# Token-major retention values, gate and memory values with 512 features per matmul

## The chip, the cores and the metric

The kernel runs on one core of one Trainium2 chip. The metric is the device time in microseconds (us) of one execution, the median of several runs. The core has five engines that work side by side, each through its own queue in order: PE (TensorE, matmuls; the profile lists its weight loads apart as PEld), DVE (VectorE), ACT (ScalarE), POOL (GpSimd) and SP (SyncE, which issues most DMAs here).

## The reference

The program is a trunk of two layers over 256 tokens of 1024 features. Each layer has a mixer (a retention branch and a convolution branch, merged by gates), a cross-attention into 256 memory tokens, and a gated MLP. What the change touches:

```python
p = u @ w_in                                  # u: 256 tokens x 1024, normalised
q, k, v, g_ret, c_in, gates = jnp.split(p, cuts, axis=-1)
...
o = head_group_norm(chunk_retention(q, k, v), ret_gn_g)   # 4 heads, 512 values each
y_a = (jax.nn.silu(g_ret) * o) @ w_ret_out
...
k, v = jnp.split(mem_n @ w_xkv, 2, axis=-1)   # 256 memory tokens, 1024 keys, 1024 values
```

The group norm ends with a gain per feature, `ret_gn_g`, that multiplies beside the gate silu(g_ret).

## The kernel before

**Arithmetic.** All large products are in float32 by three matmuls in the one-pass float type (fp32r): each operand is split into a high and a low part, and high x high, high x low and low x high are summed in PSUM. `split` (lines 160 to 163) makes the parts with one ACT copy and one DVE subtraction; for weights the same stands in `prepare` (lines 125 to 133: tiles `raw`, `whi`, `wlo`).

**Weight stream.** Weights come as chunks of 128 partitions x 2048 numbers (1 MB). A chunk is two units of 1024 columns. `run` (lines 135 to 151) goes through a list of steps; it keeps up to four units split ahead of the step in hand (`UNITS`), four chunks on their way (`RAWS`), and after each step deals out some background work, in the mixer the 31 taps of the depthwise convolution (ACT products L488, DVE sums L491, tiles `prod` and `blk`). A scheduler that estimates times sets each engine's final order from that program order; `urgent` functions go ahead.

**Two ways to multiply.** `feat` (L171 to L173) has a weight block as the stationary operand and streams 256 tokens past it, so that the result is feature-major: features on partitions, tokens along the free axis. `tok` (L181 to L183) has 128 tokens of the activation as the stationary operand and streams 256 weight columns past them: the result is token-major. A chunk takes 48 matmuls of 128x256 either way: 8 k tiles x 3 products x 2 feature or token tiles. A `tok` step needs both units of its chunk for the first token tile and both again for the second.

**PSUM.** Step results go to four rotating banks, tag `mm`, one bank (2 x 256 numbers per partition) a step.

**Retention.** For each head: chunks of q, k (`feat`), two chunks of values v (`tok`), two chunks of the gate g (`feat`, silu on eviction, L590), then `scores` and `attend` (token-major result, group norm, tile `o`), and later `gate` (lines 559 to 574): eight transposes of `o` on PE (L563), the product with gain and gate on DVE (L571), and a split into `y`.

**Cross-attention.** `mem_v` (lines 447 to 454) makes the memory values in four `tok` chunks, each evicted by a split (L162, L163) on its own, between the steps of the four attention heads.

Of the kernel before, what the change touches and what calls it, by code (L numbers as in the profile page):

```python
# [7 lines left out]
F32 = mybir.dt.float32  # L8
# [3 lines left out]
ALU = mybir.AluOpType  # L12

P = 128
# [13 lines left out]
# columns of the parameter block, per layer (the final gain follows the layers)  # L28
# [11 lines left out]
# first chunks of the parts of the input projection: q, k, v, retention gate, convolution, merge gates  # L40
Q0, K0, V0, G0, C0, S0 = 0, 4, 8, 16, 24, 32

RAWS = 4        # chunks of weights on their way from DRAM
UNITS = 4       # half chunks kept split
BLOCKS = 10     # [128, 8, 256] tiles
TEMPS = 8       # [128, 2, 256] tiles
ROT_BY = 20     # units of the first layer over which the rotary tables are made
CONV_END = 1    # chunk of the retention output by which the taps are done
MEM_AT = 6      # chunk of the retention output after which the memory is normalised
# [6 lines left out]
def urgent(fn):  # L56
    """ahead of the weights still to be split"""
    def wrapped(self, *args, **kwargs):
        with self.tc.high_priority():
            return fn(self, *args, **kwargs)  # L60
    return wrapped


class Trunk:
# [37 lines left out]
    def step(self, fn, *units):  # L102
        """units: (chunk in DRAM, first column, k tiles, columns per k tile)"""
        self.steps.append((fn, units))
        self.planned += len(units)
# [5 lines left out]
    def token_pair(self, name, layer, c):  # L111
        src = self.io[name][layer, c]
        return (src, 0, 4, 256), (src, 1024, 4, 256)
# [39 lines left out]
    def spread_out(self, by):  # L153
        """work to be spread evenly over the steps up to unit number by"""
        work = {"items": [], "by": by, "due": 0.0}
        self.background.append(work)
        return work

# [1 line left out]
    def split(self, src, hi, lo):  # L160
        """src = hi + lo exactly, both rounded to the width of one pass."""
        self.nc.scalar.activation(hi, src, AF.Copy)  # L162
        self.nc.vector.tensor_tensor(lo, src, hi.bitcast(F32), op=ALU.subtract)  # L163

    def feat(self, out, w, u, k0=0, first=True, last=True):
        """out[feature, token] += sum_k w[k, feature] u[k, token]"""
        (wh, wl), (uh, ul) = w, u
        kt = wh.shape[1]
        for k in range(kt):
            a, b = first and k == 0, last and k == kt - 1  # L170
            self.nc.tensor.matmul(out, wh[:, k, :], uh[:, k0 + k, :], start=a, stop=False)  # L171
            self.nc.tensor.matmul(out, wh[:, k, :], ul[:, k0 + k, :], start=False, stop=False)  # L172
            self.nc.tensor.matmul(out, wl[:, k, :], uh[:, k0 + k, :], start=False, stop=b)  # L173

    def tok(self, out, ws, t, u):
        """out[token, feature] = sum_k u[k, token] w[k, feature]"""
        uh, ul = u
        ts = slice(t * P, t * P + P)
        for k in range(KT):
            wh, wl = (x[:, k % 4, :] for x in ws[k // 4])  # L180
            self.nc.tensor.matmul(out, uh[:, k, ts], wh, start=k == 0, stop=False)  # L181
            self.nc.tensor.matmul(out, uh[:, k, ts], wl, start=False, stop=False)  # L182
            self.nc.tensor.matmul(out, ul[:, k, ts], wh, start=False, stop=k == KT - 1)  # L183
# [6 lines left out]
    def tok_sum(self, parts):  # L190
        """per token: sum over partitions and over the parts, tokens on partitions"""
        ps = self.bank("nrm", 1)
        for i in range(2):
            for j, t in enumerate(parts):
                self.nc.tensor.matmul(ps[:, 0, i:i + 1], t[:, i * P:i * P + P], self.ones[:, 0:1],
                                      start=j == 0, stop=j == len(parts) - 1)
        return ps

    def spread(self, pending):
        """one value per token onto every partition, tokens along the free axis"""  # L200
        ps, col = pending
        for t in range(2):
            self.nc.tensor.matmul(ps[:, 1, t * P:t * P + P], col[:, t:t + 1].to_broadcast([P, P]), self.ident,
                                  start=True, stop=True)
        return ps[:, 1, :]
# [7 lines left out]
    def ssq_add(self, k, n, h):  # L213
        """squares of n feature tiles from tile k on; those of the last pair are left to the final sum"""
        nc, q = self.nc, self.temp()
        nc.scalar.activation(q[:, :n, :], h, AF.Square)
        last = self.gain == "final"
        if last and k >= 6:
            self.ssq += [q[:, i, :] for i in range(n)]
            return  # L220
        if k and n == 2:
            a = self.temp()
            nc.vector.tensor_tensor(a, self.ssq, q, op=ALU.add)
            q = a
        elif k:
            nc.vector.tensor_tensor(self.ssq[:, k % 2, :], self.ssq[:, k % 2, :], q[:, 0, :], op=ALU.add)
            q = self.ssq
        self.ssq = [self.halves(q)] if k + n == (6 if last else KT) else q
# [4 lines left out]
    def begin(self, gain=None):  # L233
        """before a residual is produced; with a gain, h times the gain is kept split as well, for
        the products that start before the norm is known"""
# [21 lines left out]
    def both(self, ps, w, u, midway=None):  # L257
        """two feature tiles side by side, k tile by k tile"""
# [13 lines left out]
    def each(self, ps, w, u, midway=None):  # L272
        """two feature tiles side by side, one after the other"""
# [11 lines left out]
    def ahead(self, chunks, normalise):  # L285
        """the first chunks after a norm work on the gained h; their results wait for the scale"""
# [92 lines left out]
    def rotary_tables(self):  # L379
        """angle in turns, reduced exactly, then sine and cosine; a list of small pieces"""  # L380
# [17 lines left out]
        def product(part, c, most, f, r):  # L398
            """acc += the part of a turn in part * c, where |part| <= most"""
# [26 lines left out]
    def memory(self, layer):  # L426
        """normalised memory, split; K and V follow as steps"""
# [19 lines left out]
    def mem_v(self, layer, c):  # L447
        def fn(*w):
            ps = self.bank()
            for t in range(2):  # L450
                self.tok(ps[:, t, :], w, t, self.mem)
            at = slice(c * 256, c * 256 + 256)
            self.split(ps, *(by_token(x)[:, :, at] for x in self.xv))
        self.step(fn, *self.token_pair("w_xkv", layer, 4 + c))

# [1 line left out]
    def mixer(self, layer):  # L457
# [19 lines left out]
        # convolution branch: the products of a tap on ScalarE, the sums on VectorE  # L477
# [40 lines left out]
        # retention  # L518
# [19 lines left out]
        def attend(h):  # L538
            s, v = X["s", h], X["v", h]
            for n in range(2):  # L540
# [15 lines left out]
                nc.scalar.activation(o, ps, AF.Identity, scale=rs, bias=nm)  # L556
                X["o", h, n] = o

        def gate(h):
# [7 lines left out]
            for j in range(2):  # L567
                y = self.temp()
                for i in range(2):
                    f = 2 * j + i  # L570
                    nc.vector.scalar_tensor_tensor(y[:, i, :], pt[j][:, i, :],  # L571
                                                   self.par("ret_gn_g", L, 4 * h + f),
                                                   X["g", h][:, f, :], op0=ALU.mult, op1=ALU.mult)
                self.split(y, hi[b][:, r + 2 * j:r + 2 * j + 2, :], lo[b][:, r + 2 * j:r + 2 * j + 2, :])

        def v_step(h, j):
            def fn(*w):
                ps = self.bank()
                for t in range(2):
                    self.tok(ps[:, t, :], w, t, X["u"])  # L580
                if j == 0:
                    X["v", h] = self.small([2, 512], "v", bufs=1)
                nc.scalar.activation(X["v", h][:, :, j * 256:(j + 1) * 256], ps, AF.Copy)
            self.step(fn, *self.token_pair("w_in", L, V0 + 2 * h + j))

        def ev_g(h, j):
            def fn(ps):
                if j == 0:
                    X["g", h] = self.small([4, N], "g", bufs=1)
                nc.scalar.activation(X["g", h][:, 2 * j:2 * j + 2, :], ps, AF.Silu)  # L590
            return fn
# [12 lines left out]
        g = lambda h: [in_step(G0 + 2 * h + j, ev_g(h, j)) for j in range(2)]  # L604
# [19 lines left out]
        # gates  # L624
# [17 lines left out]
        # retention output  # L642
# [43 lines left out]
        # convolution output and merge  # L686
# [29 lines left out]
    def cross(self, layer):  # L716
# [19 lines left out]
        def three(out, a, b, first, last):  # L736
            """out += a.T @ b, both split"""
# [155 lines left out]
def _turns():  # L893
    """1/(2 pi) in pieces of twelve bits"""
# [106 lines left out]
```

## Time and profile before

| What | Value |
| --- | --- |
| median of 3 runs | 1309.79 us (1309.69 to 1309.8) |
| profiled execution, span from first to last instruction | 1308.2 us |
| outside the span, median less span | 1.6 us |
| PE busy | 1290.4 us (99%) |
| DVE busy | 973.9 us (74%) |
| ACT busy | 852.2 us (65%) |
| mean granted TensorE clock | 0.997 |

The page gives no time of the profiled execution but its span; the 1.6 us between it and the median is taken as what lies around the span. A matmul's row has its duration with its passage through the array; matmuls overlap, so what one costs is the distance between the starts of neighbours, read from the timeline.

### The profile page before, as it was taken

The numbers are of one execution on the slowest core, as the hardware profiler recorded it, in microseconds if no ns is written. First come the engines' busy times: TensorE is split into PE (matmuls) and PEld (weight loads), VectorE is DVE, ScalarE is ACT, GpSimd is POOL, SyncE is SP. The second block draws the span as 40 slices with busy tenths as digits, with TensorE's granted clock in tenths as the row PEclk, the third lists the DMA queues.
The fourth block names the chain that finished last, engine by engine and source line by source line (L and its number), as shares of the span: only waits on it lengthen the run. The fifth ranks groups of instructions, "written<-read, shape, count | busy, mean of one in ns | idle before, by whom it ended". The sixth has DMA issues, their size and how long they took to land.

```text
span 1308.2 us, 25199 instructions
## 1 busy us (share of the span) xinstructions
PE 1290.4 (99%) x10592; PEld 1277.0 (98%) x10592; DVE 973.9 (74%) x1283; ACT 852.2 (65%) x1348; POOL 24.0 (2%) x31
## 2 busy tenths in 40 slices
PE   7999999999999999999999999999999999999997
PEld 6999999999999999999999999999999999999997
DVE  7989998767676588665677999985686757876643
ACT  5898899664455457654469898886544545666542
POOL 0000000000000000000000010000000000000000
PEclk9999999999999999999999999999999999999998
DMA  8554445455544345454555444445645444455450
GB/s 301 197 190 142 156 155 191 165 205 182 193 166 158 131 169 212 170 182 178 187 191 175 179 146 162 154 155 191 226 164 191 164 154 153 175 193 175 158 185 33
DMA packets 33089, 227.45 MB, mean 174 GB/s; under 512 B 3920, under 2 KB 4176, under 8 KB 6736
## 3 DMA queue, kind: packets, MB, share of 16 engines
q1 hardware_dynamic: 32688, 225.32, 47.9%
q8 instruction: 83, 1.36, 0.4%
q10 hardware_dynamic: 288, 0.52, 0.1%
q14 instruction: 30, 0.25, 0.0%
HBM read 224.78 MB, written 1.05 MB: 173 GB/s over the span
## 4 chain that ended last, share of the span: by engine, by line
PE 84%; issue 14%; DMA 1%; DVE 0%; SPq 0%; POOLq 0%; POOL 0%; DVEq 0%
PE mm L171 22%; PE mm L172 22%; PE mm L173 22%; PE mm L181 4%; PE mm L183 4%; PE mm L182 4%; PE mm L266 3%; PE att L542 1%; PE att L739 1%; PE att L740 1%; PE att L738 1%; DMA h<-in_x_dram 1%; PE att L563 1%; PE att L531 1%; PE att L544 1%
## 5 line engine op out<-in xcount | busy, mean ns | idle before, releaser
L171 PE MATMUL mm<-blk,whi 128*128 128x256 f32 x2880 | 817.0, 284 | 0.0
L173 PE MATMUL mm<-blk,wlo 128*128 128x256 f32 x2880 | 814.9, 283 | 0.0
L172 PE MATMUL mm<-blk,whi 128*128 128x256 f32 x2880 | 814.8, 283 | 0.0
L130 ACT ACTIVATE whi<-raw 128x1024 fp32r<-128x1024 f32 (+1 forms) x424 | 442.9, 1048 | 376.4 <-PE mm L172 289.3
L131 DVE TENSOR_TENSOR wlo<-raw,whi 128x1024 fp32r<-128x1024 f32 (+1 forms) x424 | 511.9, 1212 | 204.6 <-ACT whi L130 202.0
L171 PEld LDWEIGHTS mm<-blk,whi 128*128 128x128 f32 x2880 | 552.0, 192 | 2.2 <-issue 1.7
L172 PEld LDWEIGHTS mm<-blk,whi 128*128 128x128 f32 x2880 | 552.2, 192 | 1.7 <-issue 1.7
L173 PEld LDWEIGHTS mm<-blk,wlo 128*128 128x128 f32 x2880 | 552.0, 192 | 0.5 <-DVE wlo L131 0.2
L488 ACT ACTIVATE prod<-blk,params 128x255 f32<-128x255 f32 (+14 forms) x480 | 197.1, 487 | 1.8 <-DVE blk L491 1.7
L491 DVE TENSOR_TENSOR blk<-blk,prod 128x1020 f32<-128x1020 f32 (+14 forms) x120 | 138.4, 1153 | 15.3 <-ACT prod L488 14.6
L182 PE MATMUL mm<-wlo,blk 128*128 128x256 f32 x384 | 109.1, 284 | 0.0
L181 PE MATMUL mm<-whi,blk 128*128 128x256 f32 x384 | 108.9, 284 | 0.0
L183 PE MATMUL mm<-whi,blk 128*128 128x256 f32 x384 | 108.6, 283 | 0.0
L183 PEld LDWEIGHTS mm<-whi,blk 128*128 128x128 f32 x384 | 73.5, 191 | 0.0
L182 PEld LDWEIGHTS mm<-wlo,blk 128*128 128x128 f32 x384 | 73.5, 191 | 0.0
L181 PEld LDWEIGHTS mm<-whi,blk 128*128 128x128 f32 x384 | 73.4, 191 | 0.0
L162 ACT ACTIVATE blk<-t 128x512 fp32r<-128x512 f32 (+1 forms) x87 | 52.1, 616 | 17.3 <-DVE t L253 12.9
L163 DVE TENSOR_TENSOR blk<-t,blk 128x512 fp32r<-128x512 f32 (+1 forms) x87 | 57.7, 678 | 2.6 <-ACT blk L162 2.6
L266 PE MATMUL mm<-blk,whi 128*128 128x256 f32 x192 | 39.7, 299 | 8.1 <-ACT whi L130 8.1
L266 PEld LDWEIGHTS mm<-blk,whi 128*128 128x128 f32 x192 | 33.1, 207 | 8.1 <-ACT whi L130 8.1
L842 DVE SCALAR_TENSOR_TENSOR t<-t,params,t 128x255 f32<-128x255 f32 (+1 forms) x88 | 38.2, 478 | 0.0
L328 DVE TENSOR_TENSOR h<-mm,h 128x512 f32<-128x512 f32 (+1 forms) x26 | 16.9, 650 | 21.1 <-PE mm L173 16.0
(133 smaller groups left out, 747.2 us busy)
## 6 DMA issues: line engine op xcount, KB each, us to landing
raw<-in_w_in_dram SPq DMA_DIRECT2D x79, 1024.0 KB, 4.8
raw<-in_w_up_dram SPq DMA_DIRECT2D x44, 1024.0 KB, 4.8
raw<-in_w_ret_out_dram SPq DMA_DIRECT2D x16, 1024.0 KB, 4.8
raw<-in_w_xkv_dram SPq DMA_DIRECT2D x16, 1024.0 KB, 4.8
raw<-in_w_down_dram SPq DMA_DIRECT2D x16, 1024.0 KB, 4.8
raw<-in_w_conv_out_dram SPq DMA_DIRECT2D x8, 1024.0 KB, 4.8
raw<-in_w_mix_out_dram SPq DMA_DIRECT2D x8, 1024.0 KB, 4.8
raw<-in_w_xq_dram SPq DMA_DIRECT2D x8, 1024.0 KB, 4.8
```

The source lines that it names most:

```text
L130: nc.scalar.activation(hi[:, :n], raw, AF.Copy)
L131: nc.vector.tensor_tensor(lo[:, :n], raw, hi[:, :n].bitcast(F32), op=ALU.subtract)
L163: self.nc.vector.tensor_tensor(lo, src, hi.bitcast(F32), op=ALU.subtract)
L171: self.nc.tensor.matmul(out, wh[:, k, :], uh[:, k0 + k, :], start=a, stop=False)
L172: self.nc.tensor.matmul(out, wh[:, k, :], ul[:, k0 + k, :], start=False, stop=False)
L173: self.nc.tensor.matmul(out, wl[:, k, :], uh[:, k0 + k, :], start=False, stop=b)
L181: self.nc.tensor.matmul(out, uh[:, k, ts], wh, start=k == 0, stop=False)
L182: self.nc.tensor.matmul(out, uh[:, k, ts], wl, start=False, stop=False)
L183: self.nc.tensor.matmul(out, ul[:, k, ts], wh, start=False, stop=k == KT - 1)
L266: mm = lambda x, y, a, b: self.nc.tensor.matmul(out, x[:, k, :], y[:, k, :], start=a, stop=b, skip_group_check=True)
L488: nc.scalar.activation(t[:, i, :m], X["c"][:, k, :m], AF.Copy, scale=self.par("conv_dw_w", L, k * TAPS + TAPS - 1 - s))
L491: nc.vector.tensor_tensor(cc, cc, t[:, :, :m], op=ALU.add)
```

## The change

Three products change; q, k, the convolution, the merge gates and all later products keep their form.

1. `tok` streams 512 weight columns per matmul, and gets both token tiles at once, each with a whole PSUM bank as its output. A chunk now holds 4 of the 8 k tiles for 512 features (was 8 k tiles for 256); two chunks make 512 features. Each takes 24 matmuls of 128x512.
2. v and the memory values use it; two banks are held over two steps, and evicted after the second one. The memory values' split therefore comes after every second chunk.
3. The retention gate g becomes token-major too (it was `feat`). The gate multiplies the normalised `o` in `attend` before the transposes, and `gate` only applies the gain while it splits: one ACT copy with a scale and one DVE instruction per 128 features.

The host lays the chunks out to match. The file also loses its comments, so that line numbers move: `feat` is L172 to L174 and `tok` L185 in the changed kernel.

```diff
-        return (src, 0, 4, 256), (src, 1024, 4, 256)
+        return (src, 0, 2, 512), (src, 1024, 2, 512)
...
-    def tok(self, out, ws, t, u):
+    def tok(self, outs, ws, u, half):
         uh, ul = u
-        ts = slice(t * P, t * P + P)
-        for k in range(KT):
-            wh, wl = (x[:, k % 4, :] for x in ws[k // 4])
-            self.nc.tensor.matmul(out, uh[:, k, ts], wh, start=k == 0, stop=False)
-            self.nc.tensor.matmul(out, uh[:, k, ts], wl, start=False, stop=False)
-            self.nc.tensor.matmul(out, ul[:, k, ts], wh, start=False, stop=k == KT - 1)
+        for i, (wh, wl) in enumerate(ws):
+            for j in range(2):
+                k = 4 * half + 2 * i + j
+                for t, out in enumerate(outs):
+                    ts = slice(t * P, t * P + P)
+                    mm = lambda a, b, p, q: self.nc.tensor.matmul(out, a[:, k, ts], b[:, j, :], start=p, stop=q)
+                    mm(uh, wh, k == 0, False)
+                    mm(uh, wl, False, False)
+                    mm(ul, wh, False, k == KT - 1)
+    def flat_banks(self):
+        return [self.bank().rearrange("p t n -> p (t n)") for _ in range(2)]
...
     def mem_v(self, layer, c):
         def fn(*w):
-            ps = self.bank()
-            for t in range(2):
-                self.tok(ps[:, t, :], w, t, self.mem)
-            at = slice(c * 256, c * 256 + 256)
-            self.split(ps, *(by_token(x)[:, :, at] for x in self.xv))
+            if c % 2 == 0:
+                self.xv_ps = self.flat_banks()
+            self.tok(self.xv_ps, w, self.mem, c % 2)
+            if c % 2:
+                at = slice(c // 2 * 512, c // 2 * 512 + 512)
+                for t in range(2):
+                    self.split(self.xv_ps[t], *(by_token(x)[:, t, at] for x in self.xv))
...
                 nc.scalar.activation(o, ps, AF.Identity, scale=rs, bias=nm)
+                nc.vector.tensor_tensor(o, o, X["g", h][:, n, :], op=ALU.mult)
...
-            for j in range(2):
-                y = self.temp()
-                for i in range(2):
-                    f = 2 * j + i
-                    nc.vector.scalar_tensor_tensor(y[:, i, :], pt[j][:, i, :],
-                                                   self.par("ret_gn_g", L, 4 * h + f),
-                                                   X["g", h][:, f, :], op0=ALU.mult, op1=ALU.mult)
-                self.split(y, hi[b][:, r + 2 * j:r + 2 * j + 2, :], lo[b][:, r + 2 * j:r + 2 * j + 2, :])
+            for f in range(4):
+                src, gain = pt[f // 2][:, f % 2, :], self.par("ret_gn_g", L, 4 * h + f)
+                yh, yl = hi[b][:, r + f, :], lo[b][:, r + f, :]
+                nc.scalar.activation(yh, src, AF.Copy, scale=gain)
+                nc.vector.scalar_tensor_tensor(yl, src, gain, yh.bitcast(F32), op0=ALU.mult, op1=ALU.subtract)
...
+        def token_step(nm, at, fun, h, j):
             def fn(*w):
                 if j == 0:
+                    X[nm, "ps"] = self.flat_banks()
+                self.tok(X[nm, "ps"], w, X["u"], j)
+                if j:
+                    X[nm, h] = self.small([2, 512], nm, bufs=1)
+                    for t in range(2):
+                        nc.scalar.activation(X[nm, h][:, t, :], X[nm, "ps"][t], fun)
+            self.step(fn, *self.token_pair("w_in", L, at + 2 * h + j))
...
-        g = lambda h: [in_step(G0 + 2 * h + j, ev_g(h, j)) for j in range(2)]
+        g = lambda h: [token_step("g", G0, AF.Silu, h, j) for j in range(2)]
```

How the order changes is shown at three places. On PE, before, at the start of the second head's values in the first layer (`mm_1383` is the PSUM bank of its first 256 features; `whi_1268`/`wlo_1269` and `whi_1272`/`wlo_1273` are the chunk's two units; `blk_322` and `blk_323` the parts of the activation):

```order
L181 MATMUL mm_1383<-whi_1268,blk_322 128x256
L182 MATMUL mm_1383<-wlo_1269,blk_322 128x256
L183 MATMUL mm_1383<-whi_1268,blk_323 128x256
...
L181 MATMUL mm_1383<-whi_1272,blk_322 128x256
L182 MATMUL mm_1383<-wlo_1273,blk_322 128x256
L183 MATMUL mm_1383<-whi_1272,blk_323 128x256
L181 MATMUL mm_1383<-whi_1268,blk_322 128x256
L182 MATMUL mm_1383<-wlo_1269,blk_322 128x256
L183 MATMUL mm_1383<-whi_1268,blk_323 128x256
```

The second unit is used up to the end of the first token tile, and then the first unit is used again for the other token tile. The same place in the changed kernel (`mm_1289` and `mm_1290` are the two token tiles' banks, `whi_1172`/`wlo_1173` and `whi_1176`/`wlo_1177` the two units):

```order
L185 MATMUL mm_1289<-whi_1172,blk_322 128x512
L185 MATMUL mm_1289<-wlo_1173,blk_322 128x512
L185 MATMUL mm_1289<-whi_1172,blk_323 128x512
L185 MATMUL mm_1290<-whi_1172,blk_322 128x512
L185 MATMUL mm_1290<-wlo_1173,blk_322 128x512
L185 MATMUL mm_1290<-whi_1172,blk_323 128x512
...
L185 MATMUL mm_1289<-whi_1176,blk_322 128x512
L185 MATMUL mm_1289<-wlo_1177,blk_322 128x512
L185 MATMUL mm_1289<-whi_1176,blk_323 128x512
```

Both token tiles take a unit before the next unit is touched, and a unit has 12 matmuls instead of 24.

On ACT, before, from the eviction of the same head's values to the split of the first head's gated output (`v_1432` the values, `prod` the tap products, `blk_745` the high part of `y`):

```order
L583 ACTIVATE v_1432<-mm_1383 128x2x256
L130 ACTIVATE whi_1452<-raw_1446 128x1024
L488 ACTIVATE prod_1672<-blk_155,params 128x232 x4
L130 ACTIVATE whi_1514<-raw_1512 128x1024
L488 ACTIVATE prod_1678<-blk_155,params 128x231 x4
L583 ACTIVATE v_1432<-mm_1456 128x2x256
L130 ACTIVATE whi_1518<-raw_1512 128x1024
L488 ACTIVATE prod_1779<-blk_155,params 128x230 x4
L162 ACTIVATE blk_745<-t_214_1532 128x512
L162 ACTIVATE blk_745<-t_215_1537 128x512
```

The same stretch on ACT in the changed kernel (`v_1361` the values, L582 the copy with the gain):

```order
L594 ACTIVATE v_1361<-mm_1289 128x512
L594 ACTIVATE v_1361<-mm_1290 128x512
L131 ACTIVATE whi_1376<-raw_1370 128x1024
L499 ACTIVATE prod_1486<-blk_155,params 128x231 x4
L131 ACTIVATE whi_1445<-raw_1443 128x1024
L499 ACTIVATE prod_1589<-blk_155,params 128x230
L582 ACTIVATE blk_745<-att_1380,params 128x256
L499 ACTIVATE prod_1589<-blk_155,params 128x230 x2
L582 ACTIVATE blk_745<-att_1381,params 128x256
```

The two evictions stand together after the second chunk, and the copies of `y` are four of 256 columns between tap products, where two of 512 stood.

On PE, in the changed kernel, at the end of the first layer's memory values (`mm_4742` and `mm_4743` their banks, `att_4840` the transposed probabilities of the last head, `mm_4881` the output projection, `att_4849` the third head's attention):

```order
L185 MATMUL mm_4743<-wlo_4715,blk_3403 128x512
L185 MATMUL mm_4743<-whi_4714,blk_3404 128x512
L773 MATMUL att_4840<-ident,t_698_4672 128x128 x4
L274 MATMUL mm_4881<-blk_4184,whi_4770 128x256
...
L274 MATMUL mm_4881<-blk_4184,wlo_4771 128x256
L744 MATMUL att_4849<-t_719_4798,blk_3427 128x256
```

In the kernel before, the third head's attention followed the transposes with nothing between; now 20 matmuls of the output projection and of the chunk after it stand there, since the values of the third head come with those of the fourth.

## Rows read from the trace of the kernel before

**Rows 1.** Page, busy time of each engine, share of the span, instructions.
```profile
PE 1290.4 (99%) x10592; PEld 1277.0 (98%) x10592; DVE 973.9 (74%) x1283; ACT 852.2 (65%) x1348; POOL 24.0 (2%) x31
```

**Rows 2.** Waits of PE: who for whom, us in total, times, longest.
```profile
PE mm L266 <- ACT whi L130: 8.1, 1, 8.1
PE mm L266 <- DVE wlo L131: 1.5, 2, 1.0
PE nrm L203 <- POOL rs_r L210: 1.1, 1, 1.1
PE nrm L195 <- ACT t L216: 0.6, 1, 0.6
```

**Rows 3.** Groups by form: line, engine, tiles, shape, count, busy us, mean ns.
```profile
L181 PE MATMUL mm<-whi,blk 128*128 128x256 f32 x384 | 108.9, 284 | 0.0
```

**Rows 4.** Timeline, first value step (start us, duration us, engine) and the step after.
```profile
60.42 0.28 PE L181 MATMUL mm<-whi,blk 128*128 128x256 f32 x1
60.42 0.19 PEld L182 LDWEIGHTS mm<-wlo,blk 128*128 128x128 f32 x1
...
71.94 0.28 PE L171 MATMUL mm<-blk,whi 128*128 128x256 f32 x1
```

**Rows 5.** Timeline, full float32 passes and transposes, back to back.
```profile
102.28 1.88 PE L542 MATMUL att<-v,sm 128*128 128x512 f32 x4
102.71 0.19 PEld L542 LDWEIGHTS att<-v,sm 128*128 128x128 f32 x1 [0.24 <-issue]
103.99 1.02 PE L544 MATMUL att<-v,sm 128*128 128x512 f32 x2
...
121.88 1.04 PE L563 MATMUL att<-ident,t 128*128 128x128 f32 x8
122.76 1.03 PE L531 MATMUL att<-q,k 128*128 128x256 f32 x4
123.62 0.61 PE L533 MATMUL att<-q,k 128*128 128x128 f32 x4
```

**Rows 6.** Groups by form: evictions and elementwise work near the edits.
```profile
L163 DVE TENSOR_TENSOR blk<-t,blk 128x512 fp32r<-128x512 f32 x85 | 56.9, 685 | 2.1 <-ACT blk L162 2.1
L162 ACT ACTIVATE blk<-t 128x512 fp32r<-128x512 f32 x85 | 51.3, 621 | 15.3 <-DVE t L253 10.8 <-DVE t L320 2.6 <-DVE t L571 1.6
L223 DVE TENSOR_TENSOR t<-t,t 128x512 f32<-128x512 f32 x25 | 17.2, 686 | 0.8 <-ACT t L216 0.6
L571 DVE SCALAR_TENSOR_TENSOR t<-att,params,g 128x256 f32<-128x256 f32 x32 | 13.5, 476 | 0.6 <-PE att L563 0.6
L632 ACT ACTIVATE blk<-mm,params 128x256 f32<-128x256 f32 x32 | 13.2, 464 | 0.0
L162 ACT ACTIVATE blk<-mm 128x512 fp32r<-128x512 f32 x16 | 9.4, 588 | 2.8 <-PE mm L183 2.8
```

**Rows 7.** Windows: both mixers' retention, first cross-attention; busy us by engine, clock, DMA share.
```profile
40.00:240.00 200.00, 200.00 (x1599) 193.82 (x1598) 182.29 (x237) 184.33 (x356) 6.70 (x8) 1.00 0.47 169
690.00:890.00 200.00, 200.00 (x1600) 193.83 (x1600) 175.18 (x219) 176.90 (x342) 7.67 (x8) 1.00 0.47 169
400.00:450.00 50.00, 50.00 (x422) 50.00 (x421) 28.62 (x45) 23.19 (x39) 0.00 (x0) 1.00 0.36 129
```

**Rows 8.** Waits of ACT, 40 to 240 us, then (behind the dots) 690 to 890 us.
```profile
ACT whi L130 <- PE mm L172: 6.2, 7, 1.8
ACT whi L130 <- PE mm L183: 5.9, 6, 1.3
...
ACT whi L130 <- PE mm L172: 12.0, 12, 2.1
ACT whi L130 <- PE mm L183: 6.9, 5, 2.2
```

**Rows 9.** Timeline where a unit's low part comes closest to its first matmul.
```profile
80.87 1.22 DVE L131 TENSOR_TENSOR wlo<-raw,whi 128x1024 fp32r<-128x1024 f32 x1
...
83.70 0.28 PE L173 MATMUL mm<-blk,wlo 128*128 128x256 f32 x1
```

More of the change, by code (lines that the diff above doesn't have):

```diff
@@ L566, in gate @@
             b, r = h // 2, (h % 2) * 4
-            for j in range(2):
-                y = self.temp()
-                for i in range(2):
-                    f = 2 * j + i
-                    nc.vector.scalar_tensor_tensor(y[:, i, :], pt[j][:, i, :],
-                                                   self.par("ret_gn_g", L, 4 * h + f),
-                                                   X["g", h][:, f, :], op0=ALU.mult, op1=ALU.mult)
-                self.split(y, hi[b][:, r + 2 * j:r + 2 * j + 2, :], lo[b][:, r + 2 * j:r + 2 * j + 2, :])
-        def v_step(h, j):
+            for f in range(4):
[4 more added lines that the diff above has]
+        def token_step(nm, at, fun, h, j):
             def fn(*w):
-                ps = self.bank()
-                for t in range(2):
-                    self.tok(ps[:, t, :], w, t, X["u"])
                 if j == 0:
[L582 to L591, printed above, removed]
+                    X[nm, "ps"] = self.flat_banks()
[5 more added lines that the diff above has]
+            self.step(fn, *self.token_pair("w_in", L, at + 2 * h + j))
+        v_step = lambda h, j: token_step("v", V0, AF.Copy, h, j)
         def ev_qk(nm, h):
@@ L942, in chunks, with token_chunks @@
         return np.ascontiguousarray(w).reshape(ll, ff // cols, P, ks * cols)
+    def token_chunks(w):
+        w = np.asarray(w)
+        ll, kk, ff = w.shape
+        w = w.reshape(ll, 2, 4, P, ff // 512, 512).transpose(0, 4, 1, 3, 2, 5)
+        return np.ascontiguousarray(w).reshape(ll, ff // 256, P, 2048)
     def mixed(w, a, b):
         w = np.asarray(w)
-        parts = [chunks(w[:, :, :a], 8, 256), chunks(w[:, :, a:b], 8, 256, "k")]
+        parts = [chunks(w[:, :, :a], 8, 256), token_chunks(w[:, :, a:b])]
         if b < w.shape[2]:
@@ L982 @@
         "decay": decay, "ident": np.eye(P, dtype=np.float32), "freq": freq,
-        "w_in": mixed(w_in, 2048, 4096), "w_ret_out": chunks(w_ret_out, 16, 128, "k"),
+        "w_in": mixed(w_in, 2048, 6144), "w_ret_out": chunks(w_ret_out, 16, 128, "k"),
         "w_conv_out": chunks(w_conv_out, 8, 256), "w_mix_out": chunks(w_mix_out, 8, 256),
```

## The prediction

> **What bounds the kernel now.** I read the busy line of the page first: PE is busy 99% of the span, DVE 74%, ACT 65% [rows 1]. A busy PE alone doesn't say that PE is the bound, so the waits of PE came next: there are four kinds, 8.1, 1.5, 1.1 and 0.6 us in total [rows 2]. The first two belong to L266, the steps that run ahead of a norm, and the last two to the norm sums; none stands in a step that the change edits. So from the first weights to the end PE takes one matmul after the other, and the time is the sum of the distances between matmul starts. The third view is the timeline of the first value step, for that distance: its 96 matmuls go from 60.42 to 71.94, that is 11.52/96 = 0.120 us each [rows 4]. (The 284 ns of a matmul's own row [rows 3] is its passage, not its price.) The last views are the windows of the two stretches in which the change sits. In the retention stretch ACT is busy 184.3 and DVE 182.3 of 200 us in the first layer, 176.9 and 175.2 in the second [rows 7]: little room. In cross-attention they take 23.2 and 28.6 of 50 [rows 7]: room enough. The granted clock is 1.00 in all three, the level of 2.4 GHz, and PE has no pause in which that would change.
>
> **PE's part.** L181 has 384 matmuls [rows 3], L182 and L183 as many: 1152 token-major ones, 768 for v and 384 for the memory values. The gate adds 16 chunks of 48 feature-major ones, 768. So 1920 matmuls of 128x256 become 960 of 128x512. What is removed is 1920 x 0.120 = 230.4 us.
>
> What a 128x512 fp32r matmul costs no row shows. Nearest are the full float32 passes: four of 128x512 start 1.71/4 = 0.428 us apart, four of 128x256 0.86/4 = 0.215 [rows 5]. They scale with the width with nothing fixed left over, and the weight side waits 0.24 us in each wide one [rows 5]: there the stream is the price. In the 256-wide fp32r matmuls it is the other way round. Each weight load starts in the same 10 ns as the matmul before it (both at 60.42 [rows 4]), and transposes of 128 columns, half the stream, still cost 0.88/8 = 0.110 [rows 5]. So a load sets a floor of 0.110 to 0.120, and an fp32r stream of 256 columns fits into it; half of the float32 pass, 0.107, would just do so. Twice that, 0.214, is what a 512-wide one costs when its load hides. Bounds: 0.120, if even 512 columns hid behind the load, and 0.428, if fp32r streamed no faster than float32. I take 0.216, a little over the stream, since its load has the whole of it to hide in, as in L542. Added: 960 x 0.216 = 207.4. PE's sum falls by 23.0 us: 8 units x (24 x 0.120 - 12 x 0.216) = 2.3 per head, 9.2 per layer, and 4.6 in the two cross-attentions.
>
> **ACT and DVE.** The evictions of v, g and the memory values keep their number of elements and of instructions (two of 512 columns where two of 2 x 256 stood): nothing. Per head, the gate's four products of 256 columns (4 x 0.476, L571) and two subtractions of 512 (2 x 0.685, L163) leave DVE, 3.27 us; two products of 512 (2 x 0.686, as L223) and four instructions of 256 (4 x 0.476) come, 3.28 [rows 6]. DVE: no change. On ACT two copies of 512 (2 x 0.621) leave and four of 256 from PSUM with a scale (4 x 0.464, as L632) come [rows 6]: 0.6 us more per head, 2.4 per layer. It lies beside PE's work, if ACT has that time.
>
> Does it? In the first layer's stretch ACT must do 2.4 us more in 9.2 us less: it needs 11.6 us of idle time. It stood idle 12.1 us because four units were split already and PE had to free one [rows 8]; that time is free to use. In the second layer 18.9 us stand against the same need [rows 8]. DVE needs 9.2 and has 17.7 and 24.8 [rows 7]. So the cover holds, by half a microsecond in the first layer: the ring of four units will be nearly empty where it was nearly full, and a late split becomes a wait of PE. The closest call before is in the first layer after the first head's q and k, where a low part ends at 82.09 and is first multiplied at 83.70 [rows 9]: 1.6 us, of which the first head's values alone take 1.15 (4 units x 0.288). Against that, a value step no longer holds both units to its end (the PE order shown), so units come free more evenly. I put 1.5 us of new PE waits on the two mixers; the bounds are 0 and the whole 18.4 saved there.
>
> **Other edits.** The product with g is added between the norm and the transposes, which stand three steps later (two for the last head, over 11 us): hidden. The four banks: a pair holds two for two steps, and the next pair takes the two that q and k left 10 us earlier; hidden by that distance. The memory values of heads 3 and 4 arrive together: two ACT copies of 0.588 and two subtractions of 0.685 [rows 6] in turn, about 2.5 us, against four transposes and 20 matmuls that the order puts there, 0.4 + 2.4 us. A split of a weight unit in between can make it late: 0 to 1.2 us a layer; I take 0.5 for both. The DMAs are as many and as large, and busy 0.47 in the stretch [rows 7]: nothing.
>
> **Sum.** Profiled span 1308.2, with the 1.6 us around it 1309.8, the median of the runs: 1309.8 - 23.0 + 1.5 + 0.5 = 1288.8 us.
>
> **Rivals.**
> ACT or DVE becomes the bound of the mixers. For it: DVE at 91% and ACT at 92% of the first stretch, and in-order queues that wait for each other. Against it: the idle time just counted. If a third to all of the mixers' 18.4 us is lost: 1295 to 1305.
>
> Part of the load stays exposed. In rows 4 a 256-wide matmul costs 0.013 more than the 0.107 of its stream. If that is a fixed toll of swapping weights, a wide one costs 0.227, the gain is 960 x 0.013 = 12.5, and the time about 1298. Against it: the wide float32 passes show no such toll [rows 5]. The Trainium skill, "TensorE: Matmul & The Clock Gate", Part 3 (The mechanism), speaks for it: weight loads overlap matmuls in flight only when they use different rows of the array. Taken whole it would put load and stream end to end, which the trace denies: both start at 60.42 [rows 4].
>
> The stream itself costs 0.120 per 256 columns. Then a wide one costs 0.240, nothing is gained on PE, and the time stays at 1310. For it: pace 0.110 at 128 columns and 0.120 at 256 is all that the rows say of fp32r. Against it: the loads' own start times.
>
> Slower: wide fp32r matmuls fall back to the float32 pace, 0.428. It is the only row of this width. The point from which the change loses is 0.240; at 0.428 the 960 matmuls add 180 us: 1490. Against it: at 256 columns fp32r takes 0.120 where float32 takes 0.215.
>
> Faster by far: 512 columns hide behind the load as 256 do, at 0.120. PE would save 1.44 us a unit; the mixers then run at ACT's pace (200 - 184.3 - 2.4 and 200 - 176.9 - 2.4, 34 us saved), the cross-attentions save 16 x 1.44 = 23: 1253. Against it: a float32 pass streams 512 columns no faster than 0.428. The Trainium skill, same page, Back-to-back issue gap, gives a sustained 131 ns for a matmul 512 wide, which would make this case; its 81 ns at 128 columns is not what transposes show here, 110 [rows 5].
>
> **Chances.** Forecast 66%, own range 1284.5 (pace 0.214, no wait) to 1293 (6 us of waits). ACT or DVE bound 14%, exposed load 9%, stream bound 5%, float32 pace 4%, load bound 2%. The range 1284 to 1301 holds the forecast, the exposed load and more than half of the second case, some 84%. A measurement of this kernel tells 0.2%, 2.6 us, from no change. Faster: 66 + 13 + 9 + 2 = 90%. Same: 5 for the stream bound and 1 of the second case, 6%. Slower: 4%.
>
> **What would show it.** In the profile after: starts of L185 matmuls 0.216 apart and PEld idle for part of each; 9600 or so PE instructions, 960 less. Waits of PE on `whi` or `wlo` in the mixers of about 1.5 us; ACT's waits for PE in 40 to 230 us nearly gone. The first mixer's end comes 8 to 9 us earlier, each cross-attention 2.3 us shorter, the rest as before. Wrong would be: L185 at 0.227 or 0.240; PE waiting for `whi` or `wlo` by 6 us or more; or waits before L744, where the memory values are read.

## The result, and the profile after

The changed kernel takes 1297.71 us (median of 4 runs, 1297.41 to 1298.12), the kernel before beside it 1309.74 (1309.35 to 1309.8). The ratio is 0.9908, with a 95% interval of 0.9894 to 0.9922: 12.0 us or 0.9% faster. The forecast was 1288.8 us in a range of 1284 to 1301. So sign and range held, and about half of the expected gain is missing. The time is that of the rival "part of the load stays exposed", which had a chance of 9% and said "about 1298".

The page of the kernel after, the row that answers to [rows 1]: busy us of each engine, share of the span (1295.7 us, 12.5 shorter), instructions.

```profile
PE 1278.4 (99%) x9632; PEld 1225.2 (95%) x9632; DVE 972.8 (75%) x1283; ACT 857.7 (66%) x1365; POOL 27.9 (2%) x31
```

PE has 960 instructions less, as forecast, but its busy time has fallen by only 12.0 us where the sum had 23.0. ACT has 5.5 us more (forecast 2 x 2.4), DVE 1.1 less (forecast none). Next, the waits of PE in the kernel after: who for whom, us in total, times, longest. This is the whole list, as [rows 2] was.

```profile
PE mm L274 <- ACT whi L131: 7.9, 1, 7.9
PE mm L274 <- DVE wlo L132: 1.1, 2, 0.7
PE nrm L211 <- POOL rs_r L218: 1.1, 1, 1.1
PE nrm L203 <- ACT t L224: 0.6, 1, 0.6
```

The same four kinds in the same places, 0.6 us less in total. None is in a step that the change edits. The forecast had put 2.0 us of new waits into the edited steps; they didn't come. So the missing gain is no wait: it must be in the distance between starts. The timeline of the first value step of the kernel after (start us, duration us, engine, line, tiles, count) answers to [rows 4]:

```profile
59.03 0.42 PEld L185 LDWEIGHTS mm<-whi,blk 128*128 128x128 f32 x2
59.26 0.62 PE L185 MATMUL mm<-whi,blk 128*128 128x512 f32 x2
59.49 0.19 PEld L185 LDWEIGHTS mm<-wlo,blk 128*128 128x128 f32 x1
59.72 0.39 PE L185 MATMUL mm<-wlo,blk 128*128 128x512 f32 x1
...
60.41 0.39 PE L185 MATMUL mm<-wlo,blk 128*128 128x512 f32 x1
...
61.09 0.39 PE L185 MATMUL mm<-wlo,blk 128*128 128x512 f32 x1
```

From one `wlo` matmul to the next are three: 59.72, 60.41, 61.09, that is 1.37/6 = 0.228 us each, and over longer stretches 0.227. The forecast had 0.216. The weight load of each starts with the matmul before it (59.49 beside 59.26 + 0.227) and is over 0.19 us later, before the next matmul starts: by the records it is hidden, as the forecast had it, and the matmul still costs 0.011 more than forecast. Over all steps the mean distance is 0.228, 0.012 over the forecast: 960 x 0.012 = 11.5 us. Left out of this mean are 25 places behind a transpose or a float32 pass, such as this one:

```profile
121.63 0.60 PE L575 MATMUL att<-ident,t 128*128 128x128 f32 x4
121.98 0.47 PE L185 MATMUL mm<-wlo,blk 128*128 128x512 f32 x1
122.30 0.39 PE L185 MATMUL mm<-whi,blk 128*128 128x512 f32 x1
```

From the first of the four transposes to the wide matmul are 0.35, three times 0.108 and then 0.03 where the last transpose should cost 0.11 too; the next start comes 0.31 later instead of 0.23. The two together, 0.34, are the prices of one transpose and one wide matmul: the surplus of 0.08 is recorded one place late, and no loss of the wide matmul.

The groups of the kernel after by form (line, engine, tiles, shape, count; busy us, mean ns; idle time before) answer to [rows 3] and, for the elementwise work, to [rows 6]:

```profile
L185 PE MATMUL mm<-whi,blk 128*128 128x512 f32 x640 | 201.9, 391 | 0.0
L185 PE MATMUL mm<-wlo,blk 128*128 128x512 f32 x320 | 128.2, 401 | 0.0
...
L583 DVE SCALAR_TENSOR_TENSOR blk<-att,params,blk 128x256 fp32r<-128x256 f32 x32 | 14.2, 474 | 0.7 <-ACT blk L582 0.7
L582 ACT ACTIVATE blk<-att,params 128x256 fp32r<-128x256 f32 x32 | 13.8, 470 | 0.1
L568 DVE TENSOR_TENSOR t<-t,g 128x512 f32<-128x512 f32 x16 | 10.9, 683 | 3.0 <-ACT t L567 3.0
```

The gate's new instructions cost what their nearest rows of before gave: 470 ns where 464 was taken, 474 for 476, 683 for 686. Last, the windows of the kernel after over the first retention stretch and the first cross-attention (busy us of PE, PEld, DVE, ACT and POOL; clock; DMA share), beside [rows 7]:

```profile
40.00:240.00 200.00, 200.00 (x1252) 178.00 (x1252) 184.35 (x240) 188.16 (x368) 10.27 (x8) 1.00 0.50 173
400.00:450.00 50.00, 50.00 (x335) 45.96 (x334) 31.62 (x46) 25.52 (x39) 0.00 (x0) 1.00 0.40 138
```

PE is busy without a gap, the clock 1.00 as before. ACT is at 94%, and its waits for PE in the first stretch, 12.1 us before [rows 8], are these now (same columns as the waits of PE):

```profile
ACT whi L131 <- PE mm L185: 5.0, 10, 1.2
ACT whi L131 <- PE mm L173: 2.5, 4, 1.4
```

7.5 us are left where the forecast had nearly none: PE came out only some 6 us earlier at the first mixer's end, not 8 to 9, so ACT still has to wait for it.

### The profile page after: what moved, and what is told of

Its sections match the earlier page's. It is cut to its first block, busy times and chain, and to the rows that moved or that the text cites. A ratio compares the mean times of both kernels' runs of the same rounds, so it can differ in the third digit from the quotient of the medians.

```text
span 1295.7 us, 23296 instructions
## 1 busy us (share of the span) xinstructions
PE 1278.4 (99%) x9632; PEld 1225.2 (95%) x9632; DVE 972.8 (75%) x1283; ACT 857.7 (66%) x1365; POOL 27.9 (2%) x31
## 3 DMA queue, kind: packets, MB, share of 16 engines
HBM read 224.78 MB, written 1.05 MB: 174 GB/s over the span
## 4 chain that ended last, share of the span: by engine, by line
PE 84%; issue 14%; DMA 0%; DVE 0%; ACT 0%; SPq 0%; POOLq 0%; POOL 0%; DVEq 0%
PE mm L172 20%; PE mm L173 20%; PE mm L174 20%; PE mm L185 17%; PE mm L274 3%; PE att L553 1%; PE att L745 1%; PE att L746 1%; PE att L744 1%; PE att L575 1%; PE att L542 1%; PE att L555 1%; PE nrm L211 0%; DMA raw<-in_w_in_dram 0%; PE nrm L203 0%
## 5 line engine op out<-in xcount | busy, mean ns | idle before, releaser
L172 PE MATMUL mm<-blk,whi 128*128 128x256 f32 x2624 | 745.4, 285 | 0.0
L173 PE MATMUL mm<-blk,whi 128*128 128x256 f32 x2624 | 742.3, 283 | 0.0
L174 PE MATMUL mm<-blk,wlo 128*128 128x256 f32 x2624 | 742.2, 283 | 0.0
L172 PEld LDWEIGHTS mm<-blk,whi 128*128 128x128 f32 x2624 | 502.8, 192 | 2.6 <-issue 1.7
L173 PEld LDWEIGHTS mm<-blk,whi 128*128 128x128 f32 x2624 | 503.0, 192 | 2.3 <-issue 2.2
L174 PEld LDWEIGHTS mm<-blk,wlo 128*128 128x128 f32 x2624 | 502.9, 192 | 0.3 <-issue 0.2
L185 PE MATMUL mm<-whi,blk 128*128 128x512 f32 x640 | 201.9, 391 | 0.0
L185 PEld LDWEIGHTS mm<-whi,blk 128*128 128x128 f32 x640 | 119.6, 188 | 25.1 <-issue 1.2
L185 PE MATMUL mm<-wlo,blk 128*128 128x512 f32 x320 | 128.2, 401 | 0.0
L185 PEld LDWEIGHTS mm<-wlo,blk 128*128 128x128 f32 x320 | 60.1, 188 | 12.8 <-issue 0.7
L163 ACT ACTIVATE blk<-t 128x512 fp32r<-128x512 f32 (+1 forms) x71 | 42.5, 614 | 16.1 <-DVE t L261 12.4
L164 DVE TENSOR_TENSOR blk<-t,blk 128x512 fp32r<-128x512 f32 (+1 forms) x71 | 47.0, 676 | 2.6 <-ACT blk L163 2.6
L274 PE MATMUL mm<-blk,whi 128*128 128x256 f32 x192 | 39.7, 295 | 7.9 <-ACT whi L131 7.9
L274 PEld LDWEIGHTS mm<-blk,whi 128*128 128x128 f32 x192 | 32.5, 201 | 7.9 <-ACT whi L131 7.9
L274 PE MATMUL mm<-blk,wlo 128*128 128x256 f32 x96 | 28.3, 295 | 1.1 <-DVE wlo L132 1.1
```

Source lines behind the costliest of these rows:

```text
L185: mm = lambda a, b, p, q: self.nc.tensor.matmul(out, a[:, k, ts], b[:, j, :], start=p, stop=q)
L274: mm = lambda x, y, a, b: self.nc.tensor.matmul(out, x[:, k, :], y[:, k, :], start=a, stop=b, skip_group_check=True)
```

## The experiments

One theory and its rivals stood at the start. The theory: a 512-wide fp32r matmul costs something fixed of 0.011 to 0.013 beside its stream, and a 256-wide one pays it as well. The rivals: the change's other parts (order, gate, banks) eat the rest; the stream itself is slower than half a float32 pass; or the load is not as hidden as it looks. "After" below is the changed kernel.

### Width alone, undone

```
for c, n in ((0, 256), (256, 256)):
    self.nc.tensor.matmul(out[:, c:c + n], a[:, k, ts], b[:, j, c:c + n], start=p and c == 0, ...)
```

> The changed kernel with each 128x512 matmul cut into two of 128x256 (same stationary tile twice); layout, gate, evictions and chunks stay as changed. Width theory (each fp32r matmul costs its stream plus about 0.013 us, so the gain of the change is 960 matmuls saved): L-numbers of tok at 0.120 a matmul, 960 x 0.013 = 12.5 us back, about 1310 us, the time of the kernel before. Rival (part of the gain comes from the new layout of the gate and the evictions): clearly below 1310, for instance 1304 if half.

Measured: 1309.34 us (10 runs, 1307.64 to 1309.73), ratio to before 1.0001 (0.9992 to 1.0011). Layout, order and gate are as in the kernel after, only each matmul of 512 is cut into two. The timeline of this kernel shows the old pace, 0.72 for six matmuls:

```profile
60.20 0.40 PE L187 MATMUL mm<-wlo,blk 128*128 128x256 f32 x2
60.44 0.64 PE L187 MATMUL mm<-whi,blk 128*128 128x256 f32 x4
60.92 0.40 PE L187 MATMUL mm<-wlo,blk 128*128 128x256 f32 x2
```

So the width brings the whole gain, 11.6 of 12.0 us, and the other edits together cost or bring nothing that can be told. The two kernels do the same arithmetic on the same data in the same places; the second has 960 matmuls more, at (1309.34 - 1297.71)/960 = 0.012 us each.

### Gate as before, the rest wide

```
-    g = lambda h: [token_step("g", G0, AF.Silu, h, j) for j in range(2)]
+    g = lambda h: [in_step(G0 + 2 * h + j, ev_g(h, j)) for j in range(2)]
```

(with the old product and split behind the transposes)

> The changed kernel with the retention gate feature-major as before (256-wide feat matmuls, gain and gate multiplied after the transposes); values and memory values stay 512 wide. Width theory: 384 of the 960 wide matmuls go back to two narrow ones, 384 x 0.013 = 5.0 us back, 1302 to 1303 us. Rival (the gate's new place costs ACT or DVE time that holds PE up): less than 5 us back, 1298 to 1300 us.

Measured: 1302.76 us (1301.55 to 1302.98), ratio 0.9948 (0.9933 to 0.9963). The gate has 768 of the 1920 matmuls and so 384 of the 960 saved. 384 x 0.013 = 5.0, and 1302.76 - 1297.71 = 5.05. Its part of the gain is its share of the matmuls, and its new place and extra ACT work cost nothing that can be told.

### Neighbouring matmuls into different banks

```
for a, b, p, q in ((uh, wh, k == 0, False), (uh, wl, False, False), (ul, wh, False, k == KT - 1)):
    for t, out in enumerate(outs):
        self.nc.tensor.matmul(out, a[:, k, t * P:t * P + P], b[:, j, :], start=p, stop=q)
```

> The changed kernel with the two token tiles taken in turn for each product, so that neighbouring matmuls write different PSUM banks (before, three in a row add into one bank). Theory that the extra 0.013 us belongs to every fp32r matmul: starts still 0.227 apart, 1297 to 1298 us. Rival (it is the cost of adding into the same bank back to back): 0.216 apart or less, 960 x 0.011 = 10 us less, 1287 us.

Measured: 1297.29 us (2 runs), ratio 0.9908 (0.9888 to 0.9928): the time of after. In the timeline of this kernel four matmuls start in 60.38 - 59.47 = 0.91 us, 0.228 each:

```profile
59.47 1.07 PE L185 MATMUL mm<-whi,blk 128*128 128x512 f32 x4
60.38 0.39 PE L185 MATMUL mm<-wlo,blk 128*128 128x512 f32 x1
```

The extra is not that one matmul adds to the sums of the one just before it.

### 512 cut into 320 and 192

```
for c, n in ((0, 320), (320, 192)): ...
```

> The changed kernel with each 512-wide matmul cut into 320 and 192 columns. Two readings of 0.120 at 256 and 0.227 at 512 columns: a fixed 0.013 plus 0.418 ns a column gives 0.146 to 0.147 for the 320 wide; 0.443 ns a column with no fixed part, and a weight load of 0.120 as the floor at 256, gives 0.142. The 192 wide: 0.110 to 0.120 by either (the floor of a load). Time: 960 x 0.03 to 0.04 more, 1327 to 1337 us.

Measured: 1327.4 us (one run), inside the expected times, but the price of each width can't be read from it. The timeline of this kernel:

```profile
61.72 0.42 PE L187 MATMUL mm<-wlo,blk 128*128 128x320 f32 x2
61.98 0.67 PE L187 MATMUL mm<-whi,blk 128*128 128x320 f32 x4
62.49 0.42 PE L187 MATMUL mm<-wlo,blk 128*128 128x320 f32 x2
62.75 0.68 PE L187 MATMUL mm<-whi,blk 128*128 128x320 f32 x4
63.27 0.42 PE L187 MATMUL mm<-wlo,blk 128*128 128x320 f32 x2
```

Twelve matmuls take 63.27 - 61.72 = 1.55, so a pair takes 0.258. But within a pair the starts stand 0.170 and 0.088 apart, and neither is the price of one matmul: 0.088 is under the 0.110 that even 128 columns cost [rows 5]. The start moves within the pair and only the sum can be read. What the sum means depends on the floor that a weight load sets under the 192 columns. The second reading in the expectation takes 0.120 for this floor, as the prediction did. The kernel before has rows that measure it, the sums of the norm, which stream one single column past a 128x128 block of four-byte numbers (its loads last 0.19, as those of fp32r do):

```profile
264.14 0.53 PEld L195 LDWEIGHTS nrm<-ones,t 128*128 128x128 f32 x4
264.26 0.50 PE L195 MATMUL nrm<-ones,t 128*128 128x1 f32 x4
264.59 0.19 PEld L172 LDWEIGHTS mm<-blk,whi 128*128 128x128 f32 x1
```

Four loads take 264.59 - 264.14 = 0.45, so the floor is 0.112. With 0.443 ns a column and nothing fixed, 256 columns would then cost 0.113; with the fixed part 0.120, and 0.120 is what they cost [rows 4]. The pair fits too, more narrowly: 0.142 + 0.112 = 0.254 without the fixed part, 0.147 + 0.112 = 0.259 with it. That a stream slows the load beside it is not seen either: transposes, with 128 columns streaming, keep to 0.110 [rows 5]. So the 0.120 of a 256-wide matmul is not the floor of its load, and what is left is a fixed extra.

### The split parts in bf16

```
-        hi = self.wp.tile([P, 1024], F32R, ...)
+        hi = self.wp.tile([P, 1024], B16, ...)
```

(so for `lo` and all the split blocks of activations)

> The changed kernel with all split operands (weights, activations, high and low parts) in bf16 instead of fp32r, so that two-byte numbers are loaded and streamed; what is left out is the lower bits of both parts. Theory that the extra 0.013 us is a price of four-byte operands (the weight load reads beside a full-rate stream): 512 wide at 0.216 or less, 256 wide at 0.107 to 0.110; PE's sum falls by 960 x 0.011 + 8160 x 0.011, about 100 us, of which the mixers, where ACT and DVE are at over 90%, can take only part: 1200 to 1240 us. Theory that every matmul with a new stationary tile pays it: 0.227 and 0.120 again, time within 5 us of 1298 us.

Measured: 1199.65 us (1199.11 to 1199.76), ratio to before 0.9162 (0.9147 to 0.9178). The timeline of this kernel, at the switch from 256 to 512 columns (some matmul records are missing, as between 56.87 and 57.30):

```profile
56.33 0.27 PE L173 MATMUL mm<-blk,whi 128*128 128x256 bf16 x1
56.44 0.27 PE L174 MATMUL mm<-blk,whi 128*128 128x256 bf16 x1
56.55 0.27 PE L175 MATMUL mm<-blk,wlo 128*128 128x256 bf16 x1
56.66 0.38 PE L186 MATMUL mm<-whi,blk 128*128 128x512 bf16 x1
56.87 0.38 PE L186 MATMUL mm<-wlo,blk 128*128 128x512 bf16 x1
57.30 0.38 PE L186 MATMUL mm<-whi,blk 128*128 128x512 bf16 x1
57.52 0.38 PE L186 MATMUL mm<-wlo,blk 128*128 128x512 bf16 x1
```

The time lies at the lower edge of what was expected. 256 columns take 0.109 (mean of all steps), 512 take (57.52 - 56.87)/3 = 0.217, 0.216 in the mean of all. That is the number of the forecast, in another type. Against fp32r the difference is 0.120 - 0.109 = 0.011 at 256 columns and 0.227 - 0.216 = 0.011 at 512: as much at either width, as a fixed price has it. A stream that is slower by the column would differ half as much at 256 as at 512, unless a load held the 256 columns back, and the floor of 0.112 shown above says that it doesn't. With both, the rival that the stream itself is slower is out. The weight side of this kernel by form, with its idle time behind the bar, shows loads of half the length:

```profile
L173 PEld LDWEIGHTS <-whi 128*128 128x128 bf16 x2624 | 256.9, 98 | 32.5 <-issue 1.5 <-ACT prod L500 0.2 <-ACT whi L132 0.2
...
L186 PEld LDWEIGHTS <-blk 128*128 128x128 bf16 x960 | 93.8, 98 | 108.9 <-issue 4.8
```

It tests a second question. PE now comes out of the first mixer 27 us earlier than before: do ACT and DVE become the bound there? ACT and DVE take as long for a split as in after (1.05 and 1.22 us for a unit's high and low part). The window of the first retention stretch (columns as above), and the waits of PE for split parts outside the steps that run ahead of a norm (L275 here), over the whole program:

```profile
40.00:210.00 170.00, 168.56 (x1077) 110.50 (x1086) 165.61 (x221) 166.44 (x330) 9.64 (x8) 1.00 0.52 183
```

```profile
PE mm L186 <- DVE wlo L133: 1.2, 3, 0.4
PE mm L174 <- DVE blk L165: 1.2, 1, 1.2
```

DVE is at 97% and ACT at 98%, and PE waits 2.4 us for them in 1198. So they nearly bound this version, but don't yet; at the pace of 0.227 there is more room. (The time is some 4 us over what the paces alone give; all waits of PE together are 14.0 us, 3.3 more than in after.)

### Half of the stationary columns

```
n = P if p else P // 2
self.nc.tensor.matmul(out[:n, :], a[:, k, t * P:t * P + n], b[:, j, :], start=p, stop=q, ...)
```

> The changed kernel in which all wide matmuls but the first of each sum load 64 columns of the stationary tile instead of 128; the sums of tokens 64 to 127 of each tile are left out but for the first product. Theory that the extra 0.013 us is the weight load reading beside the stream, in proportion to what it reads: about 0.220 apart, 960 x 0.0065 = 6 us less, 1291 to 1292 us. Theory of a fixed toll for each matmul, whatever its load: still 0.227, 1297 to 1298 us.

Measured: 1300.41 us (one run), 2.7 us over after: outside both expectations, and on the side of the fixed toll. The weight loads by form are shorter, 134 ns for 188, and the weight side stands idle far more (56.3 us before the loads of this group, 25.1 in after); the timeline of this kernel shows that the matmuls do not come faster:

```profile
L187 PEld LDWEIGHTS mm<-whi,blk 128*64 128x64 f32 x600 | 80.5, 134 | 56.3 <-issue 1.5
```

```profile
62.28 0.85 PE L187 MATMUL mm<-whi,blk 128*64 128x512 f32 x3
62.96 0.39 PE L187 MATMUL mm<-wlo,blk 128*64 128x512 f32 x1
```

Three in 0.68 us, 0.227; the mean over all steps is 0.230, where after has 0.228. A load that is 54 ns shorter gives nothing back. So the extra is not a piece of the load that sticks out.

### bf16, width undone

The bf16 kernel with the two matmuls of 256 columns of the first experiment.

> The bf16 kernel with each 128x512 matmul cut into two of 128x256; as there, the lower bits of both parts are left out. In bf16 the wide one took 0.216 and the narrow 0.109, so a matmul saved is worth 2 x 0.109 - 0.216 = 0.002 us. Theory that the width pays only by the extra of four-byte matmuls: 960 x 0.002 = 2 us over the bf16 kernel's 1199.7, about 1201 to 1202 us. Rival (fewer, longer matmuls pay by themselves, for instance since units of weights come free more evenly): 8 to 12 us over it, 1208 to 1212 us.

Measured: 1204.3 us (1204.02 to 1204.49), ratio to before 0.9197 (0.9182 to 0.9212): 4.6 us over the wide bf16 kernel, where fp32r lost 11.6. Of the 4.6, 2.4 are the pace (in the mean of all steps two of 256 take 0.2183 and one of 512 takes 0.2158: 960 x 0.0025). The waits of PE come to 16.1 us in this kernel and to 14.0 in the wide one, 2.1 more. The time lies between the two expectations, nearer the theory's 2 us than the rival's 8 to 12, and the pace is the theory's. What the width is worth is thus a matter of the type: 0.012 for each matmul saved in fp32r, 0.0025 by pace in bf16.

### Half of the rows

```
matmul(out, a[:P // 2, k, ts], b[:P // 2, j, :], start=p, stop=q)
```

> The changed kernel in which the wide matmuls use partitions 0 to 63 of both operands alone; the other half of each sum over k is left out. Half as many rows are loaded and half as many streamed, in as many columns. Theory that the extra 0.011 us of an fp32r matmul grows with the amount of four-byte numbers read from memory: 0.221 to 0.222 apart, 5 us less than the changed kernel, 1292 to 1293 us. Theory that it is a fixed price of each fp32r matmul: 0.227 again, 1297 to 1298 us.

Measured: 1313.7 us (one run; before 1309.68), that is 16 us over after, which neither side had expected. The pace within a step is unchanged, as the timeline of this kernel shows, three in 0.68:

```profile
62.40 0.84 PE L185 MATMUL mm<-whi,blk 64*128 64x512 f32 x3
63.08 0.39 PE L185 MATMUL mm<-wlo,blk 64*128 64x512 f32 x1
```

So the extra doesn't grow with the rows read either. The 16 us stand where matmuls of 64 and of 128 rows follow each other:

```profile
59.57 0.28 PE L174 MATMUL mm<-blk,wlo 128*128 128x256 f32 x1
59.78 0.50 PE L185 MATMUL mm<-whi,blk 64*128 64x512 f32 x1
60.12 0.39 PE L185 MATMUL mm<-wlo,blk 64*128 64x512 f32 x1
```

The first start behind the change comes after 0.21 instead of 0.120, the second after 0.34 instead of 0.227. There are 88 such changes, and these two starts together come 16.0 us later than in after. No wait is shown for them; why a change costs this stays open.

## Why the prediction was half right

**What bounds the kernel** held: PE without a pause, so each us saved in matmul starts is a us of the end. 1920 x 0.120 = 230.4 removed is right (narrow gives it back whole), and so is the count of 960.

**The step that failed** is the price of the wide matmul: "Twice that, 0.214, is what a 512-wide one costs when its load hides. ... I take 0.216". It measured 0.227. More exactly, it is the reading that stands ahead of it, that the full float32 passes "scale with the width with nothing fixed left over", carried over to fp32r. That is true of those passes [rows 5], but they stream at half the column rate, 0.428 for 512, and say nothing of what fp32r pays beside its stream. The row of fp32r itself said it: 0.120 for 256 columns [rows 4], 0.013 more than the 0.107 of its stream. The prediction named that excess, and explained it away as a floor set by the weight load into which 256 columns just fit. The trace of before denied this floor already, with the one-column rows of L195 at 0.112. The runs show the excess to be a price per matmul: 0.011 over bf16 at both widths, with the load cut to 134 ns, with half the rows and with another bank. Put in, the sum is 1309.8 - 960 x 0.013 = 1297.3, and measured are 1297.71. That the range held is not the forecast's merit: its own part ended at 1293, and the measured time lies in what was kept for the rivals.

The rival had the right pace, gain and time, but called the toll one "of swapping weights". That much is not shown. Matmuls that follow one with the same stationary block come at 0.227 too, but each has a load of its own, so the swap of weights and the start of a stream can't be told apart in these runs. An experiment with fp32r on one side and bf16 on the other might have done so and wasn't tried. That the toll belongs to the type is what is shown.

**The Trainium skill**, "TensorE: Matmul & The Clock Gate", section Back-to-back issue gap, was weighed for its sustained 131 ns at 512 columns. No run here shows it: the fastest was 216. The same section gives N/2.4 plus 2.5 ns for an isolated gap, 109 and 216 ns for 256 and 512 columns. The bf16 rows agree with it to the nanosecond (0.109, 0.216) in a stream of real matmuls; the fp32r rows (0.120, 0.227) stand 11 ns above. The list in Part 3 (The mechanism) of that page of the Trainium skill, which the prediction cites, has loads overlap matmuls only on other rows of the array; rows 59.26 and 59.49 above show that they overlap on the same rows too.

**The waits**, 2.0 us, were mis-sized: none came. Part of the cover was never asked for, since PE gained only half. But the bf16 run shows that also with a far faster PE only 2.4 us are lost there, so the rival "ACT or DVE becomes the bound" was too dear at 14%.

**Right in size:** ACT's and DVE's added work, the gate's new place (gateback), the four banks and the waits in cross-attention, whose L744 waits for nothing; each cross-attention is 1.1 us shorter where 2.3 were forecast, by the pace again. Of the 12.5 us in the span 11.2 are the edited steps (960 x 0.2281 = 219.0 against 1920 x 0.1199 = 230.2, means without the starts behind transposes and float32 passes) and 0.6 the shorter waits of L274; 0.7 were not assigned to a place.

The rivals "stream bound" (0.240), "float32 pace" (0.428) and "load bound" (0.120) are refuted by the row at 0.227.

## What to carry to other kernels

- Take a matmul's price from two widths of its own type before multiplying: price = columns x slope + something fixed. Halving the number of matmuls at the same columns saves the fixed part and no more; here that is 0.012 us each in fp32r and 0.0025 in bf16.
- A row of another type is a bound, not an estimate. If the nearest row of the same type shows an excess that isn't explained, carry it into the sum at its full size, and test the explanation first that makes it vanish: here a one-column row of the same trace had the floor of a load at 0.112, not 0.120.
- The larger gain lay beside this change: with both split parts in bf16 the same program takes 1199.65 us, the fastest here. It keeps fewer bits of each operand, and that is a decision on precision, not on time.

## What the runs showed of the hardware that was not expected

- An fp32r matmul costs 0.011 us more than a bf16 one at 256 and at 512 columns alike; the slope per column is the same, (0.227 - 0.120)/256 = 0.42 ns.
- The distance between two starts isn't always one matmul's price: in pairs of 320 and 192 columns it is 0.170 and 0.088, and only the sum, 0.258, says something; a wide matmul behind a transpose is recorded 0.03 behind it, though the transpose costs 0.110.
- Cutting 960 matmuls to 64 rows among others of 128 cost 16 us, 0.18 at each of 88 changes, although each read half as much.
- A weight load of 128 columns lasts 188 to 192 ns in fp32r, 98 in bf16 and 134 for 64 columns in fp32r. Loads of 0.19 follow each other every 0.112 us when only one column streams. Behind a stream of 512 fp32r columns the load of 134 brought no faster pace than that of 188.
